# Routing on 64 candidate sums a head, spread over 26 pairs of expert tiles, with all of that stretch's splits on VectorE

## The chip, the cores and the metric

The kernel runs on one core of a Trainium2 chip. TensorE (PE) multiplies, VectorE (DVE), ScalarE (ACT) and GpSimd (POOL) do the rest, and SyncE (SP) issues the transfers. The metric is the device time of one execution in microseconds (us); times below are from one profiled execution unless a median is named.

## The reference, cut to what matters

A decoder layer on 256 tokens of width 1024: a mixer (a state space model beside block attention), a layer norm, then PEER, a product-key retrieval over 128 x 128 single-neuron experts, and a last layer norm. The change lies in PEER alone:

```
q   = (xc @ w_q)                                   # 8 heads, 2 halves of 128
s   = einsum(q, sub_keys)                          # 128 scores per half
s1, i1 = top_k(s[:, :, 0], 16);  s2, i2 = top_k(s[:, :, 1], 16)
cand = s1[..., :, None] + s2[..., None, :]         # 16 x 16 sums a head
top, pos = top_k(cand, 16)                         # the 16 best of 256
eidx = (i1 * 128 + i2) at pos;   g = softmax(top)
act  = gelu(xc . expert_u[eidx]);  out = sum(g * act * expert_v[eidx])
```

Both lists of 16 are sorted, largest first. The sum at row i and column j can be among the best 16 only if (i + 1)(j + 1) is at most 16, since every sum above and to the left is at least as large.

## The kernel before, in words

The kernel does not gather experts. It multiplies the tokens with all 128 blocks of U (128 experts each), applies the gelu, multiplies each by its gate (zero where the expert was not chosen), and multiplies the result with all 128 blocks of V.

**Splits.** Float32 operands are multiplied as a rounded part `hi` and a remainder `lo`. `split` (lines 66 to 73) makes them for one 128x1024 tile: ScalarE casts `raw` to `hi` (L71), then VectorE or GpSimd subtracts (L72). The stream has four `raw` buffers (`RAWB`) and three each of `hi` and `lo` (`HIB`, `LOB`). SyncE starts the load of a tile when the `lo` four tiles earlier has been made.

**Stages of PEER, in order.**
1. 16 tiles of `w_q` give the queries and the scores; VectorE takes the 16 largest of each 128 scores (`top16`: MAX8, index search, replace, MAX8, index search).
2. The first half of U: 32 calls of `u_pair`, two tiles each, `dense` with 24 matmuls a tile (hi by xh, hi by xl, lo by xh) into one of two `psb` banks, then the gelu of the pair on ScalarE (L769). The first tile's `lo` is VectorE's, the second's GpSimd's. Beside it runs `route(b)` for the token blocks b = 0 and 1: the sums `cand`, `top16` on 256 sums for each of 8 heads, the positions split into row and column, both looked up by comparing with a counter (`eq`, L799 to L804), the exponential of the gates on ScalarE (L809, with a table load on either side), and at the end three transposes a block on TensorE into a `psb` bank (L818), from which VectorE copies `i1T`, `i2T` and `gT`.
3. The second half of U, 32 pairs, with the gate matrices built beside it: for 8 tokens at a time (a group) VectorE makes `o1`, `eq` and twice `o2` (L865 to L868) from `i1T`, `i2T`, `gT`; TensorE multiplies them (L873); VectorE and ScalarE apply the result (L880, L883). Groups 0 to 15 are block 0's tokens. GpSimd has the second tile's `lo` and a product (L909) here.
4. V: 128 tiles against the gated activations, then the last norm.

**What sets the order.** Each engine runs its instructions in the order in which they stand. A scheduler sets that order from the program's order and its own estimate of times; `issue_after` keeps what is written inside it behind a named instruction. In stage 2 one step of routing is handed out after each pair (`PACE`), and the scheduler may move steps ahead.

Of the kernel before, what the change touches and what calls it, by code (L numbers as in the profile page):

```python
# [8 lines left out]
F32 = mybir.dt.float32  # L9
F32R = mybir.dt.float32r  # L10
BF = mybir.dt.bfloat16
# [3 lines left out]
AF = mybir.ActivationFunctionType  # L15
OP = mybir.AluOpType
# [10 lines left out]
TOPK = 16  # L27
# [6 lines left out]
GSC = 2.0 ** 14  # L34
# [7 lines left out]
def f32(ap):  # L42
    return ap.bitcast(F32)
# [10 lines left out]
def layer(ctx, tc, I, out, tap=None, upto=None):  # L54
    nc = tc.nc
    V, S, P, PE = nc.vector, nc.scalar, nc.gpsimd, nc.tensor

    const = ctx.enter_context(tc.tile_pool(name="const", bufs=1))
    stream = ctx.enter_context(tc.tile_pool(name="stream", bufs=1))
    RAWB, HIB, LOB = 4, 3, 3  # L60

    def load(src):
        raw = stream.tile([128, 1024], F32, tag="raw", bufs=RAWB, name="raw")
        nc.sync.dma_start(raw, src.rearrange("p a b -> p (a b)") if len(src.shape) == 3 else src)
        return raw

    def split(raw, eng=V, hi=None, lo=None):
        if hi is None:
            hi = stream.tile([128, 1024], F32R, tag="hi", bufs=HIB, name="hi")
            lo = stream.tile([128, 1024], F32R, tag="lo", bufs=LOB, name="lo")  # L70
        S.copy(hi, raw)  # L71
        eng.tensor_tensor(lo, raw, f32(hi), op=OP.subtract)  # L72
        return hi, lo

    ident = const.tile([128, 128], F32, name="ident")
# [20 lines left out]
    def sbank(shape):  # L96
        return ps.tile(shape, F32, tag="s", bufs=2, name="psb")
# [5 lines left out]
    with ExitStack() as px:  # L103
# [6 lines left out]
        with ExitStack() as mx:  # L110
            sb = mx.enter_context(tc.tile_pool(name="sb", bufs=1))
# [610 lines left out]
    with ExitStack() as rx:  # L722
# [14 lines left out]
        PACE = lambda i: 1  # L737
        keys = sb.tile([128, 16, NK], F32, name="keys")
        nc.sync.dma_start(keys, I["keys"])

# [23 lines left out]
        def u_pair(i):  # L764
            pt = sbank([128, 2, T])
            for r in range(2):
                hi, lo = split(load(I["u"][i + r]), P if r else V)
                dense(PE, pt[:, r], hi, lo, xh, xl)
            S.activation(act[0][:, i:i + 2], pt, AF.Gelu_apprx_tanh)  # L769

        gn = sb.tile([128, 2, 128], F32, name="gn")
        i1n = sb.tile([128, 2, 128], F32, name="i1n")
        i2n = sb.tile([128, 2, 128], F32, name="i2n")

        def route(b):
# [6 lines left out]
            fv = topf.rearrange("p (h c) k -> p h c k", c=2)  # L782
            sh = [128, 8, 16, 16]
            yield V.tensor_tensor(cand, tv[:, :, 0, :, None].to_broadcast(sh),
                                  tv[:, :, 1, None, :].to_broadcast(sh), op=OP.add)
            best = sb.tile([128, 8, 16], F32, tag="best", bufs=1, name="best")
# [7 lines left out]
            V.tensor_scalar(ab[:, 0], pos, 4, None, op0=OP.logical_shift_right)  # L794
            V.tensor_scalar(ab[:, 1], pos, 15, None, op0=OP.bitwise_and)
            yield V.tensor_copy(abf, ab)
# [10 lines left out]
            df = sb.tile([128, 8, 16], F32, tag="df", bufs=1, name="df")  # L807
            V.tensor_tensor(df, best, best[:, :, 0:1].to_broadcast([128, 8, 16]), op=OP.subtract)
            S.activation(df, df, AF.Exp)  # L809
            yield  # L810
            sm = sb.tile([128, 8], F32, tag="sm", bufs=1, name="sm")
            V.tensor_reduce(sm, df, axis=AX.X, op=OP.add)
            V.reciprocal(sm, sm)
            yield V.tensor_tensor(gn[:, b].rearrange("p (h k) -> p h k", k=16), df,
                                  sm[:, :, None].to_broadcast([128, 8, 16]), op=OP.mult)
            pt = sbank([128, 3, 128])
            for i, s in enumerate((i1n, i2n, gn)):
                PE.transpose(pt[:, i], s[:, b], ident)  # L818
            sl = slice(128 * b, 128 * b + 128)
            V.tensor_copy(i1T[:, sl], pt[:, 0])  # L820
            V.tensor_copy(i2T[:, sl], pt[:, 1])

            gr = sb.tile([128, 128], F32, tag="gr", bufs=1, name="gr")
            V.tensor_scalar(gr, pt[:, 2], GSC, None, op0=OP.mult)
            V.tensor_copy(gT[:, 0, sl], gr)
            yield V.tensor_sub(gT[:, 1, sl], gr, gT[:, 0, sl])
            if tap:
                tap(f"i1n{b}", i1n[:, b]); tap(f"gn{b}", gn[:, b])
# [6 lines left out]
        for _ in routing:  # L835
            pass

    actp1 = ctx.enter_context(tc.tile_pool(name="actp1", bufs=1))
# [236 lines left out]
```

## Time and profile before

| What | us |
|---|---|
| median of 3 runs (lowest, highest) | 1005.85 (1005.19, 1007.71) |
| the profiled execution, whole | 1009.14 |
| its span, first to last instruction | 1007.4 |
| TensorE busy in the span | 965.5 |
| VectorE, ScalarE, GpSimd busy | 708.8, 453.4, 246.9 |

The busy share counts pipelined matmuls, whose records overlap; where TensorE waits, a gap stands ahead of a matmul's record, with the instruction that ended it. The first half of U lies at about 213 to 413 us of the span, the second half at 413 to about 640 us.

### The profile page before, as it was taken

The numbers are of one execution on the slowest core, as the hardware profiler recorded it, in microseconds if no ns is written. First come the engines' busy times: TensorE is split into PE (matmuls) and PEld (weight loads), VectorE is DVE, ScalarE is ACT, GpSimd is POOL, SyncE is SP. The second block draws the span as 40 slices with busy tenths as digits, with TensorE's granted clock in tenths as the row PEclk, the third lists the DMA queues.
The fourth block names the chain that finished last, engine by engine and source line by source line (L and its number), as shares of the span: only waits on it lengthen the run. The fifth ranks groups of instructions, "written<-read, shape, count | busy, mean of one in ns | idle before, by whom it ended". The sixth has DMA issues, their size and how long they took to land.

```text
span 1007.4 us, 16390 instructions
## 1 busy us (share of the span) xinstructions
PE 965.5 (96%) x6326; PEld 857.0 (85%) x6326; DVE 708.8 (70%) x1348; ACT 453.4 (45%) x736; POOL 246.9 (25%) x123
## 2 busy tenths in 40 slices
PE   7899997999889999999999999999999999999996
PEld 3776887999889999999999998978888888888884
DVE  8965577999993612597879999755555555555556
ACT  3214543545344444454444343554554455544552
POOL 2000010144543444345464564600000000000002
PEclk9999998999999999999999999999999999999998
DMA  8312354544446565544444443656666676666661
GB/s 334 105 43 63 95 178 168 162 151 149 149 145 198 167 199 173 165 147 147 147 147 122 133 145 126 209 176 199 190 190 196 196 262 202 190 199 193 191 194 55
DMA packets 46142, 166.24 MB, mean 165 GB/s; under 512 B 5232, under 2 KB 5232, under 8 KB 45936
## 3 DMA queue, kind: packets, MB, share of 16 engines
q1 hardware_dynamic: 46064, 165.20, 51.7%
q8 instruction: 49, 0.80, 0.3%
q14 instruction: 29, 0.24, 0.1%
HBM read 163.09 MB, written 2.10 MB: 164 GB/s over the span
## 4 chain that ended last, share of the span: by engine, by line
PE 71%; DVE 23%; DMA 2%; issue 1%; ACT 1%; SPq 0%; POOL 0%; DVEq 0%; ACTq 0%; POOLq 0%
PE pw L925 34%; PE psb L995 25%; DVE lo L72 5%; PE pw L162 2%; PE pw L873 2%; DVE o L868 2%; DVE act L880 2%; PE psb L151 2%; DVE tmp L732 1%; PE pw L630 1%; DVE o L865 1%; DVE topi L734 1%; DVE eq L801 1%; DMA w<-in_w_in 1%; DVE topi L731 1%
## 5 line engine op out<-in xcount | busy, mean ns | idle before, releaser
L71 ACT CAST hi<-raw 128x1024 fp32r<-128x1024 f32 x275 | 289.6, 1054 | 320.7 <-PE pw L925 164.5
L72 DVE TENSOR_TENSOR lo<-raw,hi 128x1024 fp32r<-128x1024 f32 x207 | 269.2, 1300 | 230.3 <-ACT hi L71 226.8
L72 POOL TENSOR_TENSOR lo<-raw,hi 128x1024 fp32r<-128x1024 f32 x68 | 179.6, 2643 | 184.1 <-ACT hi L71 119.0
L995 PE MATMUL psb<-xh,lo 128*128 128x256 f32 x1024 | 153.0, 289 | 9.9 <-DVE lo L72 9.5
L995 PE MATMUL psb<-xh,hi 128*128 128x256 f32 x1024 | 157.8, 290 | 2.5 <-ACT act L769 2.4
L995 PE MATMUL psb<-xl,hi 128*128 128x256 f32 x1024 | 154.3, 290 | 0.0
L925 PE MATMUL pw<-hi,wh 128*128 128x512 f32 x492 | 151.8, 389 | 1.0 <-ACT wh L845 1.0
L925 PE MATMUL pw<-hi,wl 128*128 128x512 f32 x492 | 152.1, 390 | 0.2
L925 PE MATMUL pw<-lo,wh 128*128 128x512 f32 x492 | 151.7, 389 | 0.0
L995 PEld LDWEIGHTS psb<-xh,lo 128*128 128x128 f32 x1024 | 133.5, 192 | 12.3 <-DVE lo L72 11.9
L995 PEld LDWEIGHTS psb<-xh,hi 128*128 128x128 f32 x1024 | 135.0, 191 | 4.0 <-ACT act L769 3.1
L995 PEld LDWEIGHTS psb<-xl,hi 128*128 128x128 f32 x1024 | 133.5, 192 | 0.0
L925 PEld LDWEIGHTS pw<-hi,wh 128*128 128x128 f32 x492 | 92.3, 188 | 20.5 <-ACT wh L845 1.4
L925 PEld LDWEIGHTS pw<-hi,wl 128*128 128x128 f32 x492 | 92.2, 188 | 20.3 <-DVE wl L846 1.1
L925 PEld LDWEIGHTS pw<-lo,wh 128*128 128x128 f32 x492 | 92.4, 188 | 19.1
L968 POOL TENSOR_TENSOR tail<-tail 128x512 f32<-128x512 f32 x2 | 2.5, 1294 | 345.7 <-ACT tail L967 345.7
L880 DVE SCALAR_TENSOR_TENSOR act<-pw,act 128x256 f32<-128x256 f32 x124 | 65.9, 588 | 20.3 <-PE pw L873 20.3
L883 ACT ACTIVATE act<-pw 128x256 f32<-128x256 f32 (+29 forms) x64 | 27.8, 434 | 102.3 <-DVE act L880 84.5
L873 PE MATMUL pw<-o,o 128*128 128x128 f16 x512 | 72.8, 225 | 0.7 <-DVE o L868 0.7
L909 POOL TENSOR_TENSOR act<-act,ga 128x512 f32<-128x512 f32 (+29 forms) x32 | 51.2, 1600 | 85.5 <-ACT ga L908 64.2
L868 DVE TENSOR_TENSOR o<-eq,gT 128x1024 f16<-128x1024 f16 x64 | 52.4, 855 | 0.1
L846 DVE TENSOR_TENSOR wl<-act,wh 128x256 fp32r<-128x256 f32 x123 | 51.3, 417 | 0.0
(274 smaller groups left out, 992.7 us busy)
## 6 DMA issues: line engine op xcount, KB each, us to landing
raw<-in_u SPq DMA_DIRECT2D x128, 512.0 KB, 3.6
raw<-in_v SPq DMA_DIRECT2D x128, 512.0 KB, 4.1
raw<-in_w_q SPq DMA_DIRECT2D x16, 512.0 KB, 4.1
w<-in_w_in SPq DMA_DIRECT2D x15, 512.0 KB, 8.6
raw<-in_w_out SPq DMA_DIRECT2D x8, 512.0 KB, 4.0
xT<-in_xT SPq DMA_DIRECT2D x4, 256.0 KB, 5.2
raw<-in_w_glu SPq DMA_DIRECT2D x2, 512.0 KB, 3.7
xn<-in_xn SPq DMA_DIRECT2D x2, 512.0 KB, 3.6
```

The source lines that it names most:

```text
L71: S.copy(hi, raw)
L72: eng.tensor_tensor(lo, raw, f32(hi), op=OP.subtract)
L151: PE.matmul(pt[b], xT[:, d, 128 * b:128 * b + 128], w[:, 512 * k:512 * k + 512], start=d == 0, stop=d == 7)
L162: PE.matmul(pt[m], w[:, c], xT[:, d], start=d == 0, stop=d == 7)
L846: V.tensor_sub(wl, act[half][:, i], f32(wh))
L868: V.tensor_tensor(o2[:, k], eq, over(gT[:, k, t]), op=OP.mult)
L873: PE.matmul(pt[:, i], o1[:, (q + i) // 2, :, i % 2], o2[:, k, (q + i) // 2, :, i % 2], start=k == 0, stop=k == 1)
L880: V.scalar_tensor_tensor(a, pt[:, :, HALF * h:HALF * h + n], 1.0 / GSC, a, op0=OP.mult, op1=OP.mult)
L883: S.activation(act[1][:, done:, tq].rearrange("p i t -> p t i"), pt[:, :, HALF + done:], AF.Copy, scale=1.0 / GSC)
L909: P.tensor_tensor(a[:, :, :m1], a[:, :, :m1], raw[:, :, :m1], op=OP.mult)
L925: PE.matmul(acc[b][c], x[:, tk], w[:, 512 * c:512 * c + 512], start=first and j == 0, stop=last and j == 2)
L995: PE.matmul(pt, w[:, 128 * d:128 * d + 128], x[:, d], start=n == 0 and d == 0, stop=n == 2 and d == ND - 1)
```

## The change

- `cand` holds 64 sums a head in place of 256: row 0 with 16 columns, rows 1 to 3 with 8, rows 4 to 7 with 4, rows 8 to 15 with 1. The row and the column of a position come from eleven small VectorE instructions in place of three.
- The looked-up indices stand as a full tile `fv`, made by ScalarE (two casts of 128x2048 a block), in place of a small VectorE cast `topf` that is broadcast when read.
- Both tiles of a pair in stage 2 are split by VectorE (`split3`, which also returns the subtraction); GpSimd has nothing in that stage.
- The 36 steps of routing are handed out over the first 26 pairs, each written behind the pair's second subtraction.
- The exponential, the sums and the products of both blocks are one instruction each (`weigh`), at pairs 27 to 29; the transposes of both blocks stand at the end of the stage.

```
+    def split3(raw):
+        S.copy(hi, raw)
+        return hi, lo, V.tensor_tensor(lo, raw, f32(hi), op=OP.subtract)
...
-                hi, lo = split(load(I["u"][i + r]), P if r else V)
+                hi, lo, low = split3(load(I["u"][i + r]))
...
-            topf = sb.tile([128, 16, TOPK], BF, tag="topf", bufs=1, name="topf")
-            V.tensor_copy(topf, topi[b])
-            cand = sb.tile([128, 8, 16, 16], F32, tag="c0", bufs=1, name="cand")
+            cand = sb.tile([128, 8, 64], F32, tag="c0", bufs=1, name="cand")
+            for n, (i0, i1, w, o) in enumerate(((0, 1, 16, 0), (1, 4, 8, 16), (4, 8, 4, 40), (8, 16, 1, 56))):
...
-                yield top16(best[:, h], pos[:, h], cand[:, h].rearrange("p a b -> p (a b)"), 256, "t2")
+                yield top16(best[:, b, h], pos[:, h], cand[:, h], 64, "t2")
...
             for c, dst in ((0, i1n), (1, i2n)):
+                fv = sb.tile(sh, BF, tag="fv", bufs=2, name="fv")
+                S.copy(fv, iv[:, :, c, :, None].to_broadcast(sh))
...
-                yield V.tensor_tensor(eq, eq, fv[:, :, c, :, None].to_broadcast(sh), op=OP.mult)
+                yield V.tensor_tensor(eq, eq, fv, op=OP.mult)
...
-        routing = chain(route(0), route(1))
-        for i in range(0, HALF, 2):
-            u_pair(i)
-            for _ in range(PACE(i)):
-                next(routing, None)
+        steps, last = chain(route(0), route(1)), weigh()
+        STEPS, PAIRS, GAP = 36, 26, 2
+        done = 0
+        for n in range(HALF // 2):
+            low, ac = u_pair(2 * n)
+            with tc.issue_after(low.ins), tc.issue_after(ac.ins) if n >= PAIRS else ExitStack():
+                while done < min(STEPS, -(-STEPS * (n + 1) // PAIRS)):
+                    done += 1
+                    next(steps, None)
+                if n >= PAIRS + GAP - 1:
+                    next(last, None)
```

VectorE in the first half of U, before (`best`, `pos`: a head's best sums and their positions; `lo`: a split): sixteen rows with two splits, the inner eight left out.

```order
L72 TENSOR_TENSOR lo<-raw,hi 128x1024
L734 MAX_INDEX pos<-best,tmp 128x8
L732 MATCH_REPLACE tmp<-best,cand 128x256
L730 MAX best<-cand 128x8
L733 MAX best<-tmp 128x8
...
L784 TENSOR_TENSOR cand<-tops 128x2048
L72 TENSOR_TENSOR lo<-raw,hi 128x1024
```

VectorE at the same stretch of the changed kernel, from the two splits of one pair to those of the next, with one head between them.

```order
L79 TENSOR_TENSOR lo<-raw,hi 128x1024 x2
L736 MAX best<-cand 128x8
L737 MAX_INDEX pos<-best,cand 128x8
L738 MATCH_REPLACE tmp<-best,cand 128x64
L739 MAX best<-tmp 128x8
L740 MAX_INDEX pos<-best,tmp 128x8
L79 TENSOR_TENSOR lo<-raw,hi 128x1024 x2
```

The searches of one head, or of two, now stand behind both splits of a pair; before, fourteen rows stood between a split and the next.

ScalarE at the start of the first half of U in the changed kernel: the two casts of `fv` for block 0 stand between the cast of U's tile 3 and the gelu of the first pair, ahead of the cast of tile 4.

```order
L750 COPY sco<-pw 128x128 x4
L78 CAST hi<-raw 128x1024
L822 CAST fv<-topi 128x2048 x2
L774 ACTIVATE act_1215<-psb 128x512
L78 CAST hi<-raw 128x1024 x3
L774 ACTIVATE act_1215<-psb 128x512
```

Before, nothing stood between the cast of tile 3 and those of tile 4 and the gelu but those themselves.

VectorE where the first half of U ends, before: the gate matrices of groups 0 and 1 (`o_4228` to `o_4297`) are made twelve splits ahead, and block 1's copies are followed at once by the products on the first gates.

```order
L72 TENSOR_TENSOR lo<-raw,hi 128x1024 x12
L820 CAST i1T<-psb 128x128
L821 CAST i2T<-psb 128x128
L824 TENSOR_SCALAR gr<-psb 128x128
L825 CAST gT<-gr 128x128
L826 TENSOR_TENSOR gT<-gr,gT 128x128
L880 SCALAR_TENSOR_TENSOR act_1215<-pw,act_1215 128x4x64 x2
L865 TENSOR_TENSOR o_4351<-iotaq,i1T 128x1024
L868 TENSOR_TENSOR o_4353<-eq,gT 128x1024 x2
```

The same place in the changed kernel (`L79` is the last split of the first half, `L72` a split of the second):

```order
L910 TENSOR_TENSOR o_4253<-eq,gT 128x1024 x2
L907 TENSOR_TENSOR o_4318<-iotaq,i1T 128x1024
L908 TENSOR_TENSOR eq<-iotaq,i2T 128x1024
L910 TENSOR_TENSOR o_4320<-eq,gT 128x1024 x2
L851 CAST i1T<-psb 128x128
L852 CAST i2T<-psb 128x128
L855 TENSOR_SCALAR gr<-psb 128x128
L72 TENSOR_TENSOR lo<-raw,hi 128x1024
L856 CAST gT<-gr 128x128
L922 SCALAR_TENSOR_TENSOR act_1215<-pw,act_1215 128x4x64
L857 TENSOR_TENSOR gT<-gr,gT 128x128
L908 TENSOR_TENSOR eq<-iotaq,i2T 128x1024
```

The matrices of groups 0 and 1 are now made in the last two tiles of the first half, directly ahead of block 1's copies. On TensorE the only difference is that block 0's three transposes stand before the last pair of the first half and not after its 21st pair.

## Rows read from the trace of the kernel before

**Rows 1.** The chain that ended last, by engine, share of the span.
```profile
PE 71%; DVE 23%; DMA 2%; issue 1%; ACT 1%; SPq 0%; POOL 0%; DVEq 0%; ACTq 0%; POOLq 0%
```
**Rows 2.** Busy time by stretch: PE, PEld, DVE, ACT, POOL, granted clock, DMA share, GB/s.
```profile
255.00:265.00 10.00, 8.17 (x56) 7.97 (x55) 10.00 (x14) 3.06 (x4) 6.18 (x3) 0.83 0.45 162
...
345.00:375.00 30.00, 30.00 (x252) 30.00 (x251) 11.59 (x9) 13.23 (x16) 13.07 (x6) 1.00 0.65 188
```
**Rows 3.** TensorE in order of time: start, duration, instruction, [idle before <-releaser].
```profile
216.83 1.12 PE L995 MATMUL psb<-xh,hi 128*128 128x256 f32 x8
...
257.17 1.12 PE L995 MATMUL psb<-xl,hi 128*128 128x256 f32 x8
260.11 1.22 PE L995 MATMUL psb<-xh,lo 128*128 128x256 f32 x8 [1.83 <-DVE lo L72]
...
316.93 1.12 PE L995 MATMUL psb<-xh,hi 128*128 128x256 f32 x8
...
319.81 1.12 PE L995 MATMUL psb<-xh,hi 128*128 128x256 f32 x8
...
337.09 0.27 PE L818 MATMUL psb<-ident,i1n 128*128 128x128 f32 x1
...
337.97 1.22 PE L995 MATMUL psb<-xh,hi 128*128 128x256 f32 x8 [0.39 <-ACT act L769]
...
412.95 0.27 PE L818 MATMUL psb<-ident,i1n 128*128 128x128 f32 x1
```
**Rows 4.** TensorE's waits, 100 to 420 us: total us, times, longest.
```profile
PE psb L995 <- DVE lo L72: 7.3, 6, 2.3
...
PE psb L995 <- ACT act L769: 2.4, 2, 2.0
```
**Rows 5.** VectorE in order of time, first half of U.
```profile
218.74 1.01 DVE L779 CAST topf<-topi 128x256 bf16<-128x256 uint32 x1
...
242.34 3.42 DVE L72 TENSOR_TENSOR lo<-raw,hi 128x1024 fp32r<-128x1024 f32 x1
...
297.51 4.46 DVE L801 TENSOR_TENSOR eq<-eq,topf 128x2048 bf16<-128x2048 bf16 x1
...
340.73 1.28 DVE L868 TENSOR_TENSOR o<-eq,gT 128x1024 f16<-128x1024 f16 x2
```
**Rows 6.** GpSimd in order of time.
```profile
240.24 4.44 POOL L72 TENSOR_TENSOR lo<-raw,hi 128x1024 fp32r<-128x1024 f32 x1 [2.66 <-ACT hi L71]
...
417.57 2.40 POOL L72 TENSOR_TENSOR lo<-raw,hi 128x1024 fp32r<-128x1024 f32 x1 [4.74 <-PE psb L995]
```
**Rows 7.** ScalarE in order of time, at block 0's exponential.
```profile
240.18 1.28 ACT L809 ACT_TABLE_LOAD   x1
246.40 0.31 ACT L809 ACTIVATE df<-df 128x128 f32<-128x128 f32 x1 [4.94 <-DVE df L808]
```
**Rows 8.** Groups by shape: count, busy us, mean ns of one, idle before.
```profile
L72 DVE TENSOR_TENSOR lo<-raw,hi 128x1024 fp32r<-128x1024 f32 x207 | 269.2, 1300 | 230.3 <-ACT hi L71 226.8 <-ACT vn L569 2.7 <-PE pw L162 0.4
...
L801 DVE TENSOR_TENSOR eq<-eq,topf 128x2048 bf16<-128x2048 bf16 x4 | 11.3, 2822 | 0.0
...
L730 DVE MAX8 tops<-sco 128x8 f32<-128x128 f32 x32 | 7.7, 279 | 0.0
...
L730 DVE MAX8 best<-cand 128x8 f32<-128x256 f32 x16 | 6.6, 413 | 0.0
...
L799 DVE TENSOR_TENSOR eq<-abf,iotal 128x2048 bf16<-128x2048 bf16 x4 | 4.9, 1216 | 0.1
```
**Rows 9.** The same view, ScalarE alone.
```profile
L71 ACT CAST hi<-raw 128x1024 fp32r<-128x1024 f32 x275 | 289.6, 1054 | 320.7 <-PE pw L925 164.5 <-PE psb L995 80.7 <-issue 25.2
...
L553 ACT ACTIVATE Kin<-ident 128x2048 f32<-128x2048 f32 x1 | 1.9, 1910 | 9.3 <-DVE ident L89 9.3
```
**Rows 10.** Start of the second half of U: VectorE makes group 2, in order of time.
```profile
420.44 1.28 DVE L868 TENSOR_TENSOR o<-eq,gT 128x1024 f16<-128x1024 f16 x2
```
**Rows 11.** The same place: TensorE's first matmuls on group 2, in order of time.
```profile
422.33 0.29 PE L873 MATMUL pw<-o,o 128*128 128x128 f16 x2
```

More of the change, by code (lines that the diff above doesn't have):

```diff
@@ L73, in split @@
         return hi, lo
+    def split3(raw):
+        hi, lo = (stream.tile([128, 1024], F32R, tag=t, bufs=n, name=t)
+                  for t, n in (("hi", HIB), ("lo", LOB)))
+        S.copy(hi, raw)
+        return hi, lo, V.tensor_tensor(lo, raw, f32(hi), op=OP.subtract)
     ident = const.tile([128, 128], F32, name="ident")
@@ L736, in layer @@
         EARLY = 16
-        PACE = lambda i: 1
         keys = sb.tile([128, 16, NK], F32, name="keys")
@@ L773, in layer @@
         i2n = sb.tile([128, 2, 128], F32, name="i2n")
+        best = sb.tile([128, 2, 8, 16], F32, name="best")
+        df = sb.tile([128, 2, 8, 16], F32, name="df")
         def route(b):
@@ L784, in route @@
-            yield V.tensor_tensor(cand, tv[:, :, 0, :, None].to_broadcast(sh),
-                                  tv[:, :, 1, None, :].to_broadcast(sh), op=OP.add)
-            best = sb.tile([128, 8, 16], F32, tag="best", bufs=1, name="best")
+            iv = topi[b].rearrange("p (h c) k -> p h c k", c=2)
+            for n, (i0, i1, w, o) in enumerate(((0, 1, 16, 0), (1, 4, 8, 16), (4, 8, 4, 40), (8, 16, 1, 56))):
+                sh = [128, 8, i1 - i0, w]
+                at = V.tensor_tensor(cand[:, :, o:o + (i1 - i0) * w].rearrange("p h (i j) -> p h i j", j=w),
+                                     tv[:, :, 0, i0:i1, None].to_broadcast(sh),
+                                     tv[:, :, 1, None, 0:w].to_broadcast(sh), op=OP.add)
@@ L795, in route @@
-            V.tensor_scalar(ab[:, 1], pos, 15, None, op0=OP.bitwise_and)
-            yield V.tensor_copy(abf, ab)
+            w0, w1 = (sb.tile([128, 8, 16], BF, tag=t, bufs=1, name=t) for t in ("w0", "w1"))
+            V.tensor_scalar(ab[:, 0], pos, 3, None, op0=OP.logical_shift_right)
+            V.tensor_scalar(ab[:, 1], pos, 2, None, op0=OP.logical_shift_right)
+            V.tensor_scalar(w0, ab[:, 0], 1.0, 0.0, op0=OP.subtract, op1=OP.max)
+            V.scalar_tensor_tensor(w1, ab[:, 1], 6.0, w0, op0=OP.subtract, op1=OP.max)
@@ new lines, in route @@
+            row = abf[:, 0]
+            yield V.scalar_tensor_tensor(row, pos, 48.0, w1, op0=OP.subtract, op1=OP.max)
+            V.tensor_scalar(w0, row, 8.0, 8.0, op0=OP.mult, op1=OP.add)
+            V.scalar_tensor_tensor(w0, row, 16.0, w0, op0=OP.mult, op1=OP.min)
+            V.tensor_scalar(w1, row, 4.0, 24.0, op0=OP.mult, op1=OP.add)
+            V.tensor_tensor(w0, w0, w1, op=OP.min)
+            V.scalar_tensor_tensor(w0, row, 48.0, w0, op0=OP.add, op1=OP.min)
+            yield V.tensor_tensor(abf[:, 1], pos, w0, op=OP.subtract)
@@ L797, in route @@
+            sh = [128, 8, 16, 16]
             for c, dst in ((0, i1n), (1, i2n)):
+                fv = sb.tile(sh, BF, tag="fv", bufs=2, name="fv")
+                S.copy(fv, iv[:, :, c, :, None].to_broadcast(sh))
                 eq = sb.tile(sh, BF, tag="c1", bufs=1, name="eq")
@@ L805, in route, with weigh @@
                                       eq[:, :, 1], op=OP.add)
-            df = sb.tile([128, 8, 16], F32, tag="df", bufs=1, name="df")
-            V.tensor_tensor(df, best, best[:, :, 0:1].to_broadcast([128, 8, 16]), op=OP.subtract)
+            V.tensor_tensor(df[:, b], best[:, b], best[:, b, :, 0:1].to_broadcast([128, 8, 16]),
+                            op=OP.subtract)
+            yield
+        def weigh():
             S.activation(df, df, AF.Exp)
-            yield
-            sm = sb.tile([128, 8], F32, tag="sm", bufs=1, name="sm")
+            for _ in range(2):
+                yield
+            sm = sb.tile([128, 2, 8], F32, name="sm")
@@ L812, in route @@
             V.tensor_reduce(sm, df, axis=AX.X, op=OP.add)
             V.reciprocal(sm, sm)
[L814 to L828, printed above, removed]
-        routing = chain(route(0), route(1))
-        for i in range(0, HALF, 2):
-            u_pair(i)
-            for _ in range(PACE(i)):
-                next(routing, None)
@@ L835, in layer @@
-        for _ in routing:
+            V.tensor_tensor(gn.rearrange("p b (h k) -> p b h k", k=16), df,
+                            sm[:, :, :, None].to_broadcast([128, 2, 8, 16]), op=OP.mult)
+            yield
+            for b in range(2):
+                pt = sbank([128, 3, 128])
+                for i, s in enumerate((i1n, i2n, gn)):
+                    PE.transpose(pt[:, i], s[:, b], ident)
+                sl = slice(128 * b, 128 * b + 128)
+                V.tensor_copy(i1T[:, sl], pt[:, 0])
+                V.tensor_copy(i2T[:, sl], pt[:, 1])
+                gr = sb.tile([128, 128], F32, tag="gr", bufs=1, name="gr")
+                V.tensor_scalar(gr, pt[:, 2], GSC, None, op0=OP.mult)
+                V.tensor_copy(gT[:, 0, sl], gr)
+                V.tensor_sub(gT[:, 1, sl], gr, gT[:, 0, sl])
+                if tap:
+                    tap(f"i1n{b}", i1n[:, b]); tap(f"gn{b}", gn[:, b])
+                yield
@@ new lines, in layer @@
+        steps, last = chain(route(0), route(1)), weigh()
[7 more added lines that the diff above has]
+                    next(steps, None)
+                if n == PAIRS - 1:
+                    assert next(steps, 0) == 0
+                if n >= PAIRS + GAP - 1:
+                    next(last, None)
@@ L836, in layer @@
+        for _ in last:
             pass
```

6 lines of the change are left out of this document (2 added, 4 removed).

## The prediction

> **What bounds the kernel now.** I read the page first, then the chain that ended last, then a table of busy time by stretch, and only then TensorE's own order. The chain gives TensorE 71% and VectorE 23% [rows 1]: most of the time TensorE sets the pace, and VectorE takes its place in some stages. The table shows where: from 345 to 375 us TensorE is busy for all 30 us at full clock with VectorE at 11.59, while from 255 to 265 VectorE is busy for all 10 and TensorE for 8.17 [rows 2]. Both lie in the first half of U, with the same matmuls; what differs is the routing on VectorE.
>
> TensorE's order gives the size. An undisturbed tile takes 319.81 - 316.93 = 2.88 us [rows 3], a pair 5.76. From the first matmul of tile 1 (216.83) to block 1's transposes (412.95) pass 196.12 us [rows 3]. The 63 tiles in it need 63 x 2.88 = 181.44. Block 0's transposes take 337.97 - 337.09 = 0.88, and the eight matmuls behind them 0.10 more than eight in a stream (1.22 against 1.12) [rows 3]: 0.98. What is left, 196.12 - 181.44 - 0.98 = **13.70 us**, is what the stage loses. Of it 7.3 are waits for VectorE's splits and 2.4 waits for the gelu that frees a bank [rows 4]. The other 4.0 are smaller: at the wait of 1.83 the eight matmuls began 2.94 behind the eight before them, not 0.96, so that the gap is 0.15 wider than the wait; and the mean granted clock of 255 to 265 is 0.83 [rows 2], so about a third of that stretch ran at 1.2 and not 2.4 GHz, just after TensorE's wait: 10 x 0.17 = 1.7 us.
>
> Why the splits are late is in VectorE's order: routing is packed between them, and some instructions take far longer than their kind. A split took 3.42 us at 242.34 where GpSimd's own split ran from 240.24 for 4.44, and a product 4.46 at 297.51 [rows 5, 6]; the means are 1.30 and 2.82 [rows 8]. And ScalarE, having loaded its table at 240.18, waited 4.94 us for block 0's differences, with the casts of the next tiles queued behind [rows 7].
>
> **The change part by part.**
>
> **VectorE's load.** A pair now holds two splits on VectorE, 2 x 1.30 = 2.60 [rows 8]; the mean contains stalls, so this is high. Over 26 pairs 26 x 5.76 = 149.8 us are there, less 67.6 for splits: **82.2 us of room** for the steps. Their cost, from both sides:
> - 16 heads with five instructions over 64 sums. MAX8 takes 279 ns over 128 and 413 over 256 [rows 8], so 212 on that line: 80 x 0.212 = 17.0, at most 80 x 0.279 = 22.3. The three short value loads of a head I put at one MAX8 of 128: 4.5.
> - 22 small instructions for rows and columns at no more than 0.279: 6.1.
> - four compares as before, 1.216 each [rows 8]: 4.9.
> - four products with `fv` full instead of broadcast: between 1.216 (the compare of the same size) and 2.822 [rows 8]: 4.9 to 11.3; I take the compare's.
> - 16 halving adds and lookups, eight `cand` pieces and two differences, all smaller than the compare: 0 to 31.6; I take half, 15.8.
>
> Together 53 us, at most 80.8. Even the upper end fits in 82.2, so VectorE's added work lies beside TensorE's and costs nothing at the end. One pair may exceed 5.76: a compare and a product at 2.82 make 4.04, with the splits 6.64. Three `lo` buffers hide it: `lo` may be written from two tiles (5.76 us) before its tile begins, and is read only after two thirds of its matmuls (1.92). If that cover is gone, such a pair costs 0.88.
>
> The product is where a page bears. The Trainium skill ("VectorE: DVE Perf Modes", "Mode 2×_1P — pack two bf16 into one 32-bit read") has tensor_tensor produce two results a cycle when all its tensors are 16-bit with neighbouring elements, and gives 1224 ns against 2293. No row here has such a product; by the page the four take 4.9, by the broadcast row 11.3, and the room is enough by either.
>
> **GpSimd silent.** With it go the long instructions of [rows 5, 6]. The 13.70 should go whole: the load is spread, no split stands behind more than a pair's steps, and neither GpSimd nor an early exponential holds VectorE or ScalarE. Late next is the stream itself: from 345 to 375 the loads kept up at 188 GB/s with TensorE never idle [rows 2].
>
> **The casts of `fv` at the start.** Two stand on ScalarE ahead of the first gelu and of the cast of tile 4, and wait for block 0's indices. Before, those were there when `topf` was cast, at 218.74 [rows 5]. VectorE now has tile 1's split ahead of them too: 218.74 + 1.30 = 220.04. A ScalarE pass over 2048 columns took 1.91 [rows 9], two 3.82: 223.86. The gelu of 512 columns lies between 0.31 (128 columns, rows 7) and 1.05 (1024, rows 9); I take 0.6: 224.46. The cast of tile 4, 1.05: 225.51. TensorE wants it at 216.83 + 3 x 2.88 = 225.47 [rows 3]. That is a loss of about 0; if an integer read through a broadcast costs half as much again it is 1.9. I take **0.3**. It can't be a gain, for TensorE has no wait there to lose. The later two casts meet full buffers and cost nothing.
>
> **One exponential.** ScalarE needs 2 x 1.05 + 0.6 = 2.7 of a pair's 5.76; two table loads (1.28 each) and an exponential (0.31 for 128 columns, under twice that for 256) [rows 7] take 3.2 against 3.06 idle, once, with three `hi` buffers in hand: 0. Its operand is made pairs earlier, so the wait of 4.94 is gone. If the differences came late all the same, the casts behind would stall as they do now.
>
> **The transposes** move, and cost the same 0.98.
>
> **The start of the second half.** Groups 0 and 1 lose their lead. Before, group 0's matrices were ready at 340.73 + 1.28 = 342.01, which is 4.92 behind block 0's transposes (337.09) [rows 3, 5], and the instructions between are the same now. TensorE reaches the gates one pair later, 5.76 + 0.98 = 6.74: group 0 is in time. Group 2 was ready at 420.44 + 1.28 = 421.72 and read at 422.33, 0.61 to spare [rows 10, 11]. Now a split (1.30) and a compare (1.28 / 2 = 0.64 for that size, rows 10) have come ahead of it: late by 1.30 + 0.64 - 0.61 = 1.33. At best idle time of VectorE swallows that: 0. At worst GpSimd's split of 2.40 [rows 6] holds VectorE for groups 2 and 3: 1.33 + 4.8 = 6.1. I take **1.3**, nearest to the counted rows.
>
> **The sum.** -13.70 + 0.3 + 1.3 = -12.1. The profiled execution took 1009.14 (span 1007.4 and 1.74 around it): 997.0. The median of the runs shown is 3.29 lower. If that lies outside this stage, the median goes to 1005.85 - 12.1 = 993.8; if the profiled run merely lost more here, to 997.0. I take 994.5.
>
> **The rivals.**
>
> *GpSimd's lock at the second half's start.* Groups 0 to 3 are made while GpSimd splits, and VectorE is held each time. For it: a split that took 3.42 instead of 1.30 [rows 5, 8] lost 2.1. Against it: only two groups have no margin. Price: 6.1, and 1.9 at the start: 1005.85 - 13.70 + 8.0 = 1000.2. The Trainium skill ("SBUF — State Buffer", "Who interferes with whom") says that VectorE, reading two tensors from SBUF, and GpSimd, reading there, exclude each other for a whole instruction; the 3.42 agrees, and by the rule the two groups lose 2 x 2.40. Chance 0.18.
>
> *The loads are the limit.* Then the splits wait for data, the waits stay, and the time with them: 1005.85 + 1.6 = 1007.4 at worst, within 0.3%. For it: only 162 GB/s from 255 to 265. Against it: the transfer engines were busy for 0.45 there, and for 0.65 at 188 GB/s where nothing waited [rows 2]. Chance 0.05.
>
> *VectorE becomes the bound, and the kernel slower.* Place: the 26 pairs. The searches of one head depend each on the one before, and now often stand alone, where two heads alternated. Every us beyond the room of 82.2 is one us lost, and from 82.2 + 12.1 + 3 = 97.3 the kernel is slower. If some 160 instructions each waited 0.3 more (a whole MAX8), the steps come to 53 + 48 = 101, 18.8 over the room, so 1005.85 - 12.1 + 18.8 = 1012.6. Against it: my upper end already prices each instruction at its full recorded length. Chance 0.04.
>
> **How the numbers follow.** The forecast has 0.70, with its own range of 991.5 (1005.19 - 13.70, no new cost) to 997.5. With the lock at 0.18 the range becomes 990.5 to 1000.5; outside lie the loads, VectorE as the bound, and 0.03 for more gain than counted. A measurement of this kernel tells about 0.3% (3 us) from no change. Faster: 0.70 + 0.18 + 0.03 = 0.91; same 0.05; slower 0.04.
>
> **What would show it.** Right: TensorE near 10 of 10 in every stretch from 217 to 399, tiles 2.88 apart, the last transposes near 399 and not 413, granted clock 1.00 throughout, VectorE about two thirds busy there, no product with `fv` above 1.3, and one or two waits of TensorE for `o` between 400 and 425. Wrong: waits for `lo` that stay; a wait for `hi` above 1 us near 225; a VectorE without idle time through the 26 pairs; or more than 3 us of waits at the second half's start.

## The result, and the profile after

The changed kernel takes **995.83 us** in the median of 4 runs, the kernel before 1006.78 in the runs beside it: a ratio of 0.9896, 95% interval [0.9869, 0.9923]. The forecast was 994.5, range 990.5 to 1000.5. The profiled run took 995.63 (span 993.8), where that of before took 1009.14 (span 1007.4).

The chain that ended last, which answers to [rows 1]:

```profile
PE 83%; DVE 14%; issue 1%; DMA 1%; ACT 0%; DVEq 0%; ACTq 0%; SPq 0%
```

TensorE's share went from 71% to 83%, VectorE's from 23% to 14%. The two stretches of [rows 2], busy time of each engine, granted clock, DMA share and GB/s:

```profile
core 0: us, PE busy (x) PEld busy (x) DVE busy (x) ACT busy (x) POOL busy (x), PEclk, DMA share, GB/s
255.00:265.00 10.00, 10.00 (x86) 10.00 (x85) 6.33 (x9) 6.08 (x6) 0.00 (x0) 1.00 0.58 164
345.00:375.00 30.00, 30.00 (x253) 30.00 (x252) 15.82 (x18) 14.23 (x17) 0.00 (x0) 1.00 0.58 180
```

From 255 to 265 TensorE had been busy 8.17 of 10 at a clock of 0.83; now it is full at 1.00, VectorE has room and GpSimd is silent. TensorE in order of time, against [rows 3]:

```profile
216.00 1.12 PE L1037 MATMUL psb<-xh,hi 128*128 128x256 f32 x8
...
391.68 0.27 PE L849 MATMUL psb<-ident,i1n 128*128 128x128 f32 x1
...
392.53 1.22 PE L1037 MATMUL psb<-xh,hi 128*128 128x256 f32 x8 [0.36 <-ACT act L774]
...
398.39 0.27 PE L849 MATMUL psb<-ident,i1n 128*128 128x128 f32 x1
```

From tile 1 to block 1's transposes pass 398.39 - 216.00 = 182.39 us, where 181.44 + 0.98 = 182.42 was worked out for a stage that loses nothing. It had been 196.12: 13.73 us are gone. TensorE's waits from 100 to 420, against [rows 4]:

```profile
PE pw L915 <- DVE o L910: 0.4, 1, 0.4
PE psb L1037 <- ACT act L774: 0.4, 1, 0.4
```

No wait for a split is left; the 0.4 for the gelu (`act`) stands behind block 0's transposes and is part of the 0.98. In what follows **loss** is always this one reading of a trace, from the first matmul of tile 1 to block 1's transposes, less 182.42. It comes from the one profiled execution of each kernel, and is sharper than the whole time: among runs of kernels that are alike up to there, tile 1 began anywhere from 215.22 to 218.87.

### The profile page after: what moved, and what is told of

Same layout as the page of the kernel before. It is cut to its first block, busy times and chain, and to the rows that moved or that the text cites. A ratio compares the mean times of both kernels' runs of the same rounds, so it can differ in the third digit from the quotient of the medians.

```text
span 993.8 us, 16409 instructions
## 1 busy us (share of the span) xinstructions
PE 962.3 (97%) x6326; PEld 855.4 (86%) x6326; DVE 713.3 (72%) x1397; ACT 458.2 (46%) x737; POOL 158.6 (16%) x91
## 4 chain that ended last, share of the span: by engine, by line
PE 83%; DVE 14%; issue 1%; DMA 1%; ACT 0%; DVEq 0%; ACTq 0%; SPq 0%
PE pw L967 34%; PE psb L1037 30%; PE pa L1037 5%; DVE lo L72 3%; PE pw L168 2%; DVE o L910 2%; DVE act L922 2%; PE pw L915 2%; PE pw L636 2%; PE psb L157 2%; DVE o L907 1%; PE pw L512 1%; PE pw L749 1%; DVE eq L908 1%; PE pw L387 1%
## 5 line engine op out<-in xcount | busy, mean ns | idle before, releaser
L72 DVE TENSOR_TENSOR lo<-raw,hi 128x1024 fp32r<-128x1024 f32 x175 | 228.1, 1303 | 157.3 <-ACT hi L71 154.2
L72 POOL TENSOR_TENSOR lo<-raw,hi 128x1024 fp32r<-128x1024 f32 x36 | 91.6, 2545 | 257.9 <-ACT hi L71 214.4
L79 DVE TENSOR_TENSOR lo<-raw,hi 128x1024 fp32r<-128x1024 f32 x64 | 78.0, 1221 | 57.3 <-ACT hi L78 57.3
```

Source lines behind the costliest of these rows:

```text
L79: return hi, lo, V.tensor_tensor(lo, raw, f32(hi), op=OP.subtract)
```

## The experiments

Runs 1, 4 and 6 edit the kernel before, all others the kernel after; the code shown is cut, and `...` stands for lines of an edit that are left out. "Rule" is the `issue_after(low.ins)` that puts a pair's steps behind that pair's split on VectorE. A **hold** is an instruction on VectorE that takes longer than its kind because it ends only about when a split on GpSimd has ended.

| run | rule | GpSimd splits | sums | loss, us | median, us | ratio to before |
|---|---|---|---|---|---|---|
| before | no | yes | 256 | 13.70 | | |
| after | yes | no | 64 | 0.0 | 995.83 | 0.9896 |
| 1 | no | no | 256 | 1.23 | 996.3 | 0.9851 [0.9828, 0.9875] |
| 2 | yes | yes | 64 | 0.0 | 995.73 | 0.9864 [0.9844, 0.9884] |
| 3 | yes | no | 256 | 1.06 | 995.87 | 0.9856 [0.9840, 0.9872] |
| 4 | no | yes | 64 | 14.85 | 1012.06 | 1.0017 [1.0002, 1.0031] |
| 5 | yes | yes | 256 | 0.0 | 995.3 | 0.9866 [0.9839, 0.9894] |
| 6 | no | no (left out) | 256 | 1.82 | 999.15 | 0.9900 [0.9861, 0.9938] |
| 7 | no | yes | 64 | 9.97 | 1006.59 | 0.9978 [0.9957, 0.9999] |
| 9 | no | no | 64 | 0.52 | 996.93 | 0.9875 [0.9850, 0.9901] |

Losses: run 1 is 401.60 - 217.95 - 182.42, run 2 398.43 - 216.01, run 3 402.34 - 218.86, run 4 412.72 - 215.45, run 5 397.64 - 215.22, run 6 400.68 - 216.44, run 7 409.44 - 217.05, run 9 401.81 - 218.87, each less 182.42.

**1. Before, GpSimd silent.**
```
-                hi, lo = split(load(I["u"][i + r]), P if r else V)
+                hi, lo = split(load(I["u"][i + r]))
```


> The kernel before with one edit: the second tile of a pair in the first half of U is split on VectorE too, so GpSimd is silent in that stage; routing stays as it was (256 sums a head, an exponential per block, steps packed one after another between the splits). The number to read is the stage's loss: from the first matmul of tile 1 to block 1's transposes, less 63 x 2.88 and 0.98 (before: 13.70; after: 0). Theory 'GpSimd' (its splits hold VectorE, and that is the loss): the loss falls under 4 us, the time by about 10. Theory 'order' (the splits stand behind packed routing steps, and that is the loss, GpSimd only lengthens some of them): VectorE has 32 more splits of 1.22 to 1.30 and each stands behind the same packs, so the loss stays at 10 or grows, and the time is within 4 us of before.

Loss 1.23, of which 0.99 is one wait for a split. This one argument, left away in the kernel before, brings 12.5 of the 13.7 us. VectorE has 32 splits more and is full from 215 to 315, and yet TensorE hardly waits, as one stretch of the table shows:

```profile
255.00:275.00 20.00, 20.00 (x169) 20.00 (x168) 20.00 (x33) 10.65 (x13) 0.00 (x0) 1.00 0.63 193
```

A VectorE that is busy throughout is thus not the cause. The theory "order" in its plain form falls.

**2. After, GpSimd's splits back.**
```
+    def split3(raw, eng=V):
...
-                hi, lo, low = split3(load(I["u"][i + r]))
+                hi, lo, at = split3(load(I["u"][i + r]), P if r else V)
+                low = low if r else at
```


> The kernel after with one edit: the second tile of each pair in the first half of U is split on GpSimd again, as before; the 64 sums, the steps behind the split (now the pair's one on VectorE) and the one exponential stay. Theory 'GpSimd': the loss comes back, 5 us or more of the 13.7, with long VectorE instructions beside GpSimd's 2.40. Theory 'order': VectorE gives 26 splits of 1.22 (32 us) to GpSimd and is held at most 26 x 2.40 = 62 us, 30 more of a room in which 37 are left, so the splits still come in time: loss under 2 us, time within 2 us of after.

Loss 0. So the theory "GpSimd" in its plain form falls too: with the steps in their place its splits cost nothing.

**3. After, 256 sums** (the `cand`, the searches and the decode of before, in the steps of after).
```
...
-                yield top16(best[:, b, h], pos[:, h], cand[:, h], 64, "t2")
+                yield top16(best[:, b, h], pos[:, h], cand[:, h].rearrange("p a b -> p (a b)"), 256, "t2")
...
```


> The kernel after with one edit: all 256 sums a head instead of 64 (one instruction makes them, the searches go over 256 columns, and the position is taken apart with a shift and a mask as before). VectorE gets 80 searches of 0.41 in place of 0.216, 15.7 us more, and two sums of 2048 columns against eight pieces. Theory 'load' (the 64 sums are what makes the steps fit): the loss comes back in part, 3 us or more. Theory 'room' (82 us of VectorE beside 26 pairs, about 45 used): 61 to 65 fit too, the loss stays under 0.5 us and the time within 1 us of after.

Loss 1.06, more than the 0.5 of "room", less than the 3 of "load"; two waits for splits of 0.24 and 0.26 at 227 and 236 are in it. The 64 sums bring at most 1 us here.

**4. Before, 64 sums** (the `cand`, the searches and the decode of after, in the steps of before).
```
...
-                yield top16(best[:, h], pos[:, h], cand[:, h].rearrange("p a b -> p (a b)"), 256, "t2")
+                yield top16(best[:, h], pos[:, h], cand[:, h], 64, "t2")
...
```


> The kernel before with one edit: 64 sums a head and the lookup of row and column that goes with them; GpSimd's splits, the packed steps, the product with the broadcast index and an exponential per block stay. Theory 'load': VectorE's packs shrink by some 15 us in all, and the loss falls by more than half, under 7 us. Theories 'order' and 'GpSimd': the packs still stand ahead of the splits and GpSimd still holds them, loss 8 to 13 us, time at most 5 us under before.

Loss 14.85, above the 8 to 13 expected, and no faster than before: less routing alone brings nothing. TensorE waits for three splits of VectorE, 8.2 us in all. The first of them, in order of time on VectorE:

```profile
234.42 2.28 DVE L815 TENSOR_TENSOR eq<-eq,topf 128x2048 bf16<-128x2048 bf16 x1
...
236.62 3.38 DVE L72 TENSOR_TENSOR lo<-raw,hi 128x1024 fp32r<-128x1024 f32 x1
```

on GpSimd:

```profile
234.49 4.44 POOL L72 TENSOR_TENSOR lo<-raw,hi 128x1024 fp32r<-128x1024 f32 x1 [1.37 <-ACT hi L71]
```

and on TensorE:

```profile
240.06 1.22 PE L1009 MATMUL psb<-xh,lo 128*128 128x256 f32 x8 [2.37 <-DVE lo L72]
```

VectorE's split, ready behind a product, gets through only when GpSimd's has ended (234.49 + 4.44 = 238.93), and takes 1.07 from there; TensorE has stood for 2.37 when it gets the tile. GpSimd's own split, started at 234.49, took 4.44 instead of 2.40: it waited for VectorE's product, which ended at 236.70.

**5. After, 256 sums and GpSimd's splits** (the edits of 2 and 3 together).

> The kernel after with 256 sums a head and GpSimd's split of every second tile, both as before; what stays of the change is the place of the steps (a pair's steps behind its split on VectorE, spread over 26 pairs) and the one exponential. If the place of the steps is enough by itself: loss of the stage under 1.5 us, TensorE without waits for lo above 1 us, time within 3 us of after. If GpSimd's splits cost whatever the order, and the 64 sums had hidden it with GpSimd back: VectorE, held up to 2.40 us in each pair, has 5.76 - 1.22 - 2.40 = 2.1 us a pair for some 2.4 us of steps, and the loss is 5 us or more.

Loss 0: what this run keeps of the change (the steps in their place, `fv` in full, one exponential) is enough, without the 64 sums and with GpSimd's splits. The holds are there. VectorE's splits in order of time:

```profile
228.65 1.94 DVE L79 TENSOR_TENSOR lo<-raw,hi 128x1024 fp32r<-128x1024 f32 x1
...
233.34 3.01 DVE L79 TENSOR_TENSOR lo<-raw,hi 128x1024 fp32r<-128x1024 f32 x1
...
238.52 1.21 DVE L79 TENSOR_TENSOR lo<-raw,hi 128x1024 fp32r<-128x1024 f32 x1
...
243.46 1.21 DVE L79 TENSOR_TENSOR lo<-raw,hi 128x1024 fp32r<-128x1024 f32 x1
```

and the split on GpSimd beside the second of them:

```profile
232.87 2.40 POOL L79 TENSOR_TENSOR lo<-raw,hi 128x1024 fp32r<-128x1024 f32 x1 [3.35 <-ACT hi L78]
```

The split at 233.34 waits out GpSimd's (to 235.27). But each of these splits stands 4.7 to 5.2 us behind the one before, less than the 5.76 in which TensorE uses one, and from 247.27 on they come 5.76 apart (once 6.54, made up by the next at 4.98): a hold takes slack and not TensorE's time.

**6. Before, the second tile's low part left out.**
```
-                hi, lo = split(load(I["u"][i + r]), P if r else V)
+                raw = load(I["u"][i + r])
+                if r:
+                    hi = lo = stream.tile([128, 1024], F32R, tag="hi", bufs=HIB, name="hi")
+                    S.copy(hi, raw)
+                else:
+                    hi, lo = split(raw)
```


> The kernel before; left out is the low part of the second tile of each pair in the first half of U (the matmuls of that third read the high part in its place, as many and as large as before), so GpSimd has nothing to do there and VectorE has no more than before: its order is that of before as far as the split of the other tile goes. If VectorE's packs alone make the first tile's split late ('order'): the waits for lo of the VectorE splits (7.1 us in 6 in the kernel before) stay at 4 or more and the stage loses 7 us or more. If GpSimd's hold is what makes the packs too long ('GpSimd'): the loss is under 3 us, with the split and the product at 1.2 and 2.3 us each.

The kernel leaves that part out of its result. Loss 1.82: waits of 0.56 for a `hi`, 0.76 for a split and the usual 0.36 behind the transposes. The same packs of routing without GpSimd beside them are nearly harmless.

**7. After, GpSimd's splits back, without the rule** (run 2's edit, and:)
```
-            with tc.issue_after(low.ins), tc.issue_after(ac.ins) if n >= PAIRS else ExitStack():
+            with tc.issue_after(ac.ins) if n >= PAIRS else ExitStack():
```


> The kernel after with GpSimd's split of every second tile, and without the rule that a pair's steps come behind that pair's split; 64 sums, 36 steps over 26 pairs and the one exponential stay. If the order on VectorE is what made GpSimd harmless in the run with GpSimd back: the loss returns, 5 us or more, with waits for lo. If 64 sums and handing the steps over 26 pairs do it: loss under 2 us. The gelu's waits (2.4 us of the loss before) should be gone either way, since no exponential stands early.

Loss 9.97: against run 2, taking out the rule alone makes it. TensorE waits 2.1 us for splits and 4.2 for the gelu (0.39 of it the usual one behind the transposes), and from 245 to 275, between and behind these waits, its mean granted clock is 0.89 (part of the stretch at 1.2 and not 2.4 GHz), which is 30 x 0.11 = 3.3 us more:

```profile
245.00:275.00 30.00, 26.09 (x188) 25.49 (x188) 29.62 (x91) 13.39 (x15) 11.24 (x5) 0.89 0.41 140
```

First the splits. VectorE's order shows that the splits are no longer 5 us apart:

```profile
245.46 1.21 DVE L79 TENSOR_TENSOR lo<-raw,hi 128x1024 fp32r<-128x1024 f32 x1
...
252.39 3.08 DVE L79 TENSOR_TENSOR lo<-raw,hi 128x1024 fp32r<-128x1024 f32 x1
...
257.86 2.48 DVE L811 SCALAR_TENSOR_TENSOR abf<-pos,w 128x128 bf16<-128x128 uint32 x1
...
263.07 1.21 DVE L79 TENSOR_TENSOR lo<-raw,hi 128x1024 fp32r<-128x1024 f32 x1
```

TensorE, which needs the last of them:

```profile
264.34 1.27 PE L1038 MATMUL psb<-xh,lo 128*128 128x256 f32 x8 [1.95 <-DVE lo L79]
```

From 252.39 to 263.07 are 10.7 us, with two holds in them (3.08 for 1.21, and 2.48 for an instruction that takes 0.28 at 233.82), and TensorE waits 1.95. One expectation failed: the gelu's waits were to be gone, and are 4.2 us. ScalarE's order shows why:

```profile
237.01 1.90 ACT L823 CAST fv<-topi 128x2048 bf16<-128x2048 uint32 x1 [5.22 <-DVE eq L827]
238.81 0.59 ACT L775 ACTIVATE act<-psb 128x512 f32<-128x512 f32 x1
```

and TensorE's, which waits for that gelu:

```profile
239.46 1.21 PE L1038 MATMUL psb<-xh,hi 128*128 128x256 f32 x8 [2.09 <-ACT act L775]
```

A cast of `fv` that came early waits 5.22 for VectorE's product, which must free its buffer, and the gelu that frees TensorE's bank stands behind it. It is the stall of the early exponential in [rows 7] with another instruction at the head. A second such cast waits 3.48, and there a hold stands in the path: the product took 3.22 for 1.21, and TensorE waits 1.76.

```profile
241.52 3.22 DVE L827 TENSOR_TENSOR eq<-eq,fv 128x2048 bf16<-128x2048 bf16 x1
```

```profile
247.22 1.21 PE L1038 MATMUL psb<-xh,hi 128*128 128x256 f32 x8 [1.76 <-ACT act L775]
```

For the first cast that is not shown: its product was not held, and how much of the 2.09 comes from holds before it and how much from the place of the cast in ScalarE's order stays open.

**8. After, two more instructions a pair.**
```
+        pad = sb.tile([128, 1024], F32, name="pad")
...
+                for _ in range(2 if n < PAIRS else 0):
+                    V.tensor_tensor(pad, pad, pad, op=OP.mult)
```


> The kernel after with two more instructions a pair on VectorE in the 26 pairs, each the size of a split (128 x 1024, f32, 1.22 us, 1.13 from one to the next), on a tile that nothing reads: 52 x 1.13 to 1.22 = 59 to 63 us more. VectorE was busy 102.6 of 150 us there, so 47.4 are free. If the room is what the prediction takes it for, the stage loses the excess, 11 to 16 us, and VectorE has no idle time in the 26 pairs; with the buffers' slack of a pair or two at the end it may be 3 less. If the three lo buffers and the order leave less than the whole room usable, it loses more than 20; if the pads only fill gaps that the routing leaves unused, less than 5.

The busy times from 215 to 365, columns as above:

```profile
215.00:245.00 30.00, 28.26 (x223) 28.05 (x222) 30.00 (x103) 14.94 (x15) 0.00 (x0) 0.94 0.41 136
...
215.00:365.00 150.00, 147.35 (x1212) 146.74 (x1211) 150.00 (x317) 71.89 (x79) 0.00 (x0) 0.99 0.52 169
```

Loss 403.84 - 216.56 - 182.42 = 4.86 (999.11 us, 0.9904 [0.9876, 0.9931]): a miss, the expectation had 11 to 16. VectorE is full for all 150 us, as expected, but more fits than counted. The added instructions (pads) take 52 x 1.13 = 58.8, so about 54 us fit beside the steps, not 47.4. The 47.4 counted every split that stands alone at its full 1.22, while back to back they start 1.13 apart; and VectorE stays full to 372.77, beyond the stretch counted. Part of the 4.86 is no wait but TensorE's clock: from 215 to 245, where the first wait for a split (1.74) lies, the mean granted clock is 0.94, and 30 x 0.06 = 1.8 us.

**9. After, without the rule** (the edit of 7 alone; GpSimd silent).

> The kernel after without the rule that a pair's steps come behind that pair's split (GpSimd silent, 64 sums, 36 steps over 26 pairs, one exponential, all as after). So far the loss of the stage needs two things at once: routing packed ahead of the splits, and GpSimd's hold (13.70 and 9.97 with both; 1.23 to 1.82 with the packs alone; 0 with GpSimd alone). If that holds, this run loses 0.5 to 3 us, most of it where ScalarE's casts of fv stand early in its queue and wait for VectorE's products, and the time is within 4 us of after. If the rule on the order is what counts in this version whatever GpSimd does, the loss is that of the run with GpSimd back, 8 us or more.

Loss 0.52. ScalarE's casts of `fv` wait for VectorE's products here too (4.77 and 2.09), but they stand elsewhere in its order, one gelu later, and TensorE does not notice. With GpSimd silent the rule is worth half a us.

**10. After, an exponential for each block.**
```
+            S.activation(df[:, b], df[:, b], AF.Exp)
             yield
...
         def weigh():
-            S.activation(df, df, AF.Exp)
```


> The kernel after with an exponential for each block of 128 tokens, inside the routing, as before, in place of one for both. ScalarE gets two more table loads of 1.28 and one more exponential of 0.4, and may wait for block 0's differences with the casts of the next tiles behind it, as it did for 4.94 us before. If the early exponential was a cost of its own: TensorE waits for gelu or hi for 1 us or more near 300, loss 1.5 us or more. If three hi buffers and the order take it up: loss under 0.5 us.

Loss 398.60 - 216.21 - 182.42 = -0.03, none (993.92 us, 0.9861 [0.9836, 0.9885]). The first exponential waited 0.19 for its operand, not 4.94.

**11 and 12. After, the transposes two pairs earlier, and the groups of gates over 28 or 26 pairs.**
```
-        STEPS, PAIRS, GAP = 36, 26, 2
+        STEPS, PAIRS, GAP = 36, 24, 2
...
-            due = spread(n, T // GT, HALF // 2 - 2)
+            due = spread(n, T // GT, HALF // 2 - 4)
```
(and `- 6` in run 12.)

> The kernel after with two edits: the 36 steps over 24 pairs and not 26, so that the transposes come two pairs earlier and groups 0 and 1 of the gates are made while GpSimd is still silent; and the 32 groups of gates handed out over 28 of the second half's 32 pairs and not 30, since VectorE has 25 of 30 us busy early there and 30 of 30 late. The room takes 24 pairs easily (54 us were left over in the run with pads). Expected: TensorE's waits for o at 398 to 410 gone (0.8 us) and of the 3.3 us lost between 515 and 605 about half back: 1 to 3 us under after. If the later loss is the price of groups whose eviction grows whatever their pace, only the 0.8: within 1 us of after.

> As the run before it, with the 32 groups over 26 pairs. A group then comes every 0.81 pairs instead of 0.94: VectorE's load early in the second half goes from 25.2 of 30 us to about 28.5, late groups have fewer columns of the second half to evict. If VectorE's late load is the limit: 2 to 4 us under after, with TensorE full from 515 to 605. If a pair with two groups in it already overruns 5.76 us early on, TensorE waits for o or lo between 410 and 500 instead, and the time is that of after or up to 3 us more.

Run 11 takes 996.19 (0.9887 [0.9863, 0.9911]), run 12 1006.22 (0.9975 [0.9957, 0.9994]). The start of the second half of U, by the table of stretches, in the kernel after:

```profile
395.00:425.00 30.00, 29.43 (x266) 27.60 (x264) 29.90 (x45) 14.48 (x23) 13.74 (x7) 1.00 0.40 124
```

and in run 11:

```profile
395.00:425.00 30.00, 30.00 (x272) 28.65 (x270) 22.70 (x32) 15.27 (x24) 11.84 (x7) 1.00 0.46 142
```

What the start lost is gone in run 11, but the time is that of the kernel after, so the gain of 1 to 3 us did not come. TensorE's waits from 395 to 625 are 3.2 us in the kernel after, 3.1 in run 11 and 10.5 in run 12. VectorE is full from 515 on in the kernel after:

```profile
515.00:545.00 30.00, 29.33 (x266) 27.52 (x265) 29.93 (x39) 13.04 (x25) 15.75 (x8) 1.00 0.39 124
```

and from 455 on in run 12:

```profile
455.00:485.00 30.00, 27.59 (x249) 25.65 (x248) 29.93 (x42) 14.07 (x25) 15.74 (x8) 1.00 0.40 123
```

A faster pace of groups moves VectorE's late load forward and does not lessen it. The 10 us by which run 12 lies above the kernel after were expected by neither theory. No run here beats the kernel after by more than the runs can tell.

## Why the prediction was right

**The loss of the stage.** 13.70 us were to go whole, and 13.73 went. Its parts were read with one slip: the 2.4 of waits for the gelu hold the 0.39 behind block 0's transposes, which is in the 0.98 already, so that 2.0 belongs to the loss and 4.4, not 4.0, is the smaller rest. That the clock's share would come back with the waits is borne out: 1.00 in every stretch, with no wait ahead of it.

**What took it away.** The prediction named causes side by side, routing packed between the splits, GpSimd's hold and the early exponential, and took all as removed. The table shows how the first two are tied: each is nearly harmless alone (runs 1, 6, 9: 0.5 to 1.8; runs 2, 5: 0), and together they lose 10 to 15 (before, runs 4, 7). That a pack of routing uses up the slack of the three `lo` buffers, so that a hold then falls on TensorE, is read from the rows of runs 4, 5 and 7; no run changed the number of buffers. In run 7 part of the loss goes through ScalarE's queue instead. So the kernel after removes the loss twice over: a silent GpSimd alone does it but for 1.23 (run 1), and so does the rest of the change with GpSimd's splits and 256 sums (run 5). The rule by itself in the kernel before was not run. The forecast needed only that one of the two did it, and could not tell them apart.

**VectorE's load.** Forecast 53 us of steps, at most 80.8 (the parts add up to 80.7). The rows of the same stage from 218 to 368, against [rows 8] (busy us, mean ns):

```profile
L79 DVE TENSOR_TENSOR lo<-raw,hi 128x1024 fp32r<-128x1024 f32 x53 | 64.6, 1222 | 45.2 <-ACT hi L78 45.2
L826 DVE TENSOR_TENSOR eq<-eq,fv 128x2048 bf16<-128x2048 bf16 x4 | 4.9, 1221 | 0.1
...
L736 DVE MAX8 best<-cand 128x8 f32<-128x64 f32 x16 | 3.1, 218 | 0.0
...
L828 DVE TENSOR_TENSOR eq<-eq 128x1024 bf16<-128x1024 bf16 x4 | 2.7, 684 | 0.0
```

The search over 64 takes 0.218 (forecast 0.212), the product 1.221: of the bounds 1.216 and 2.822 the lower. The Trainium skill ("VectorE: DVE Perf Modes", "The perf-mode tier table (the rule you actually need)") gives 1224 ns for a tensor_tensor of 2048 bf16 elements; the trace agrees with 1221. All steps come to about 46 and not 53; the term that was too large is the half taken for the adds, lookups and sums (15.8, measured 9.6). It changed nothing, since the room was far from used up: run 3 put in 256 sums for a loss of 1.06, run 8 another 58.8 us for 4.86.

**The casts of `fv` at the start.** Forecast 0.3, measured 0. ScalarE in order of time:

```profile
216.82 1.90 ACT L822 CAST fv<-topi 128x2048 bf16<-128x2048 uint32 x1 [0.54 <-DVE topi L740]
218.89 1.90 ACT L822 CAST fv<-topi 128x2048 bf16<-128x2048 uint32 x1 [0.18 <-DVE topi L740]
220.70 0.59 ACT L774 ACTIVATE act<-psb 128x512 f32<-128x512 f32 x1
221.19 1.99 ACT L78 CAST hi<-raw 128x1024 fp32r<-128x1024 f32 x2
```

The pass of 1.90 was right (1.91). The step that failed is when the indices are there: the first cast began at 216.82 and the second at 218.89, each released by an index search, where both were to begin behind 220.04. TensorE wanted tile 4 at 216.00 + 8.64 = 224.64, by which time the casts of tile 4 and of the next were over (223.18). That the later two casts cost nothing holds with the steps in place or with GpSimd silent (run 9), and not in run 7.

**One exponential.** Forecast 0. It ran at 376.51 for 0.42 with no wait on TensorE. Run 10 goes further: two exponentials cost nothing either. What had stalled ScalarE was not their number but that one stood in its queue before its operand was made. The prediction showed block 0's wait of 4.94, behind which TensorE waits for no gelu; the one that cost something is block 1's. In the kernel before, ScalarE:

```profile
283.96 0.31 ACT L809 ACTIVATE df<-df 128x128 f32<-128x128 f32 x1 [3.95 <-DVE df L808]
```

and TensorE behind it:

```profile
286.23 1.21 PE L995 MATMUL psb<-xh,hi 128*128 128x256 f32 x8 [1.97 <-ACT act L769]
```

This is the 2.0 of [rows 4].

**The start of the second half.** Forecast 1.3. Measured from block 1's transposes to a matching matmul: 413.24 - 398.39 = 14.85, before 427.03 - 412.95 = 14.08, so 0.77. VectorE's order there:

```profile
397.80 3.37 DVE L910 TENSOR_TENSOR o<-eq,gT 128x1024 f16<-128x1024 f16 x2
...
403.59 1.93 DVE L857 TENSOR_TENSOR gT<-gr,gT 128x128 f16<-128x128 f32 x1
```

GpSimd's:

```profile
395.92 4.09 POOL L72 TENSOR_TENSOR lo<-raw,hi 128x1024 fp32r<-128x1024 f32 x1 [191.04 <-ACT hi L71]
402.97 2.40 POOL L72 TENSOR_TENSOR lo<-raw,hi 128x1024 fp32r<-128x1024 f32 x1 [2.96 <-ACT hi L71]
```

and TensorE's first wait:

```profile
408.62 0.22 PE L915 MATMUL pw<-o,o 128*128 128x128 f16 x1 [0.37 <-DVE o L910]
```

The rival of GpSimd's lock is in these rows: 1.93 for an instruction of 0.28, and 3.37 for a pair that takes 1.28. Its mechanism was right and its price of 6.1 was not: VectorE was held for 3.7 us there and TensorE lost 0.77, so the groups had more slack than the reading of group 2 gave. The rival that the loads are the limit is out (ScalarE has no wait for `raw` in the first half of U, DMA share 0.58). In the kernel before ScalarE did wait for `raw` there, five times and 14.0 us in all (total us, times, longest, from 205 to 340):

```profile
ACT hi L71 <- DMA raw<-in_u: 14.0, 5, 4.4
```

SyncE starts a load only when an earlier `lo` has been made, so late splits make late loads, and with the splits in time these waits are gone. And VectorE is not the bound: even with 58.8 us more (run 8) the kernel stays faster than before.

**The sum.** From profiled run to profiled run the span fell by 13.6: 13.73 in the stage, less 0.77, with tile 1 0.83 earlier (nothing in the forecast, and well within the spread of runs) and some 0.2 lost elsewhere. The medians differ by only 10.95, since the profiled run of before (1009.14) lies above the runs timed beside the changed kernel (1005.19 to 1008.49). The 43 runs of before beside the experiments have medians of 1009.47, 1009.01 and 1008.98, so the first four lay low and the change is worth about 13 us; the ratios of runs 2 and 5 (0.9864, 0.9866), which lose nothing in the stage either, say the same. The choice of 994.5 was 1.3 low. That it came so near is in part luck: it was chosen between 993.8 and 997.0, and the change alone was forecast at 12.1 where the profiled runs differ by 13.5.

## What to carry to other kernels

In this kernel the holds between VectorE and GpSimd cost nothing while the splits had slack, and the order of the queue spent that slack: before taking an engine out of a stage, look how far apart the instructions stand that the bound engine waits for, against the time in which it uses one. Put fillers behind them, one portion at a time, and the total of the filling hardly matters (58.8 us more on VectorE cost 4.86). Measure such a stage from its own first to its own last instruction; here that told 0.5 us where the whole time told 3.

## What the runs showed of the hardware

VectorE's searches pass beside a split on GpSimd unhindered, while another instruction with one tensor operand can be held. In run 5 the split on GpSimd at 227.11 (2.40) saw searches of 0.40 to 0.41 beside it, and beside the one at 244.39 (2.54) stood, in VectorE's order of run 5,

```profile
244.58 2.43 DVE L802 TENSOR_SCALAR ab<-pos 128x128 uint32<-128x128 uint32 x1
246.93 0.21 DVE L803 TENSOR_SCALAR ab<-pos 128x128 uint32<-128x128 uint32 x1
```

the next of its kind taking 0.21. The Trainium skill ("SBUF — State Buffer", "Who interferes with whom") has tensor_scalar able to enter modes that take the port pair shared with GpSimd, and leaves instructions with a single input outside those modes free; the searches and the row of 2.43 agree with that. The prediction had weighed only the clause on two inputs.
